# An encoder layer: order of expert loads, home of the one-hot tile, halves of a norm, place of the ranking, two slots, and steps of the attention list

## The chip, the cores and the metric

The kernel runs on one core of a Trainium2 chip. The metric is the device time of one execution in microseconds (us), as the median of three runs. Everything below speaks of the one core's engines: TensorE (PE; PEld is its loading of weights), VectorE (DVE), ScalarE (ACT), GpSimd (POOL), and SyncE (SP), on whose queue the loads of weights are issued.

## What is computed

One bidirectional encoder layer on 256 tokens of width 1024, in f32. From the reference, cut down:

```python
h = x @ w_in                                   # one projection, cut into six
qa, ka, va, qb, kb, vb = split(h)              # A: 8 heads on 2 kv heads; B: 4 differential heads
out_a = softmax(rope2d(rms(qa)) @ rope2d(rms(ka)).T / 8) @ va
p = softmax(rope(qb) @ rope(kb).T / 8)         # two maps per head
out_b = rms((p[:, :, 0] - lam * p[:, :, 1]) @ vb) * (1 - lambda_init)
x = LN(alpha * x + concat(out_a, out_b) @ w_mix_out)
x = LN(alpha * x + memory_cross_attention(x, mem, w_mem_q, w_mem_kv, w_mem_out))   # 4 heads, 256 memory tokens
logits = x @ w_router + b_router
top_v, top_i = top_k(logits, 4)                # 4 of 32 experts for each token
combine = one_hot(top_i) * softmax(top_v)
for e in range(32):
    g, u = x @ w_g[e] + b_g[e], x @ w_u[e] + b_u[e]        # 1024 x 1024 each
    g, u = min(g, 7), clip(u, -7, 7)
    y += combine[:, e] * ((g * sigmoid(1.702 * g) * (u + 1)) @ w_d[e] + b_d[e])
x = LN(alpha * x + y)
```

Each expert has three matrices of 4 MiB (gate, up, down), so the 32 experts are 384 MiB that must come from the chip's memory once.

## The kernel before

**Slots and pairs.** Weights stand in twenty places of 128 x 2048 f32 (1 MiB each), the slots; slots 2p and 2p + 1 together are pair p and can hold one load of 2 MiB. `free` (L117) lists the slots that are free, in the order in which they came free, at first 0 to 19. `take` (L132) takes the first of the list, `give` (L135) puts slots at its end, and `take_pair` (L141) takes the pair that has been complete for longest (`pairs`, L138). So the order of the list at the start, the order of the loads and the order in which tiles are used settle which load waits for which readers. Early work lies in slots too: the attention carves its tiles out of some, and other tiles come out of a slot named by hand. In the rows below, `sw` is a 1 MiB slot, `sp` a pair, `swh` and `srh` are half a slot with the projections' weights and their split parts.

**The loads.** There are two lists of loads in `queues` (L147 and on): the half loads of the projections, and the line of all other loads, which for the experts is put together at L336 to L340. For expert x it takes gate (`g_`), then the down matrix of the expert before (`d_`), then up (`u_`). `emit` (L207) gives a load its slot and issues it on SP, `pump` (L224) issues for as long as there is room. SP issues in order: a load whose slot is still being read holds all that stand behind it. The first two experts are fixed (NSTATIC = 2); their loads, and the gate and up of the third, are of 1 MiB, nearly all later ones of 2 MiB. Which experts come third and later is found at run time: they are ranked by the number of their tokens, and SP reads each rank's id with `values_load` (L332) before the first load of it. At the third expert (x == NSTATIC) the line before reads `*d_[:3], *g_, d_[3], *u_`: three down loads of expert 1, the four gate loads of the third, the fourth down load.

**The attention.** A planner is not used; the order of the attention's steps on TensorE, VectorE and ScalarE is written out by hand in `SEQ` (L49), one word for each step: `split` casts a weight tile and subtracts (on VectorE or, with G, on GpSimd), `proj,b..` is a projection, `rq` and `rB` are rotations of queries and keys, `rms` the reciprocal roots (L673), `qt` and `qB` and `kB` transpositions (L694), `S,c,h` scores and softmax exponentials (L700, L813), `N,c,h` the division of a block of scores by its sum (L705, L709), `T,c` the transposition of such a block with its copies (L712, L842 to L845), `V,c` the product with the values (L717, L722). Scores, transpositions and products share the four PSUM banks `ps` (L150), the projections four others (`pa`).

**The routing.** After the cross-attention, x2 (the tile `x_home`) is normed in two blocks of 128 tokens, `norm_part(c)` (L1063), one VectorE instruction each for all 1024 columns. `first_oh(c)` (L1087) makes the one-hot matrix that sorts a block's tokens to the first two experts; it is the tile `oh0` (L1085), half of a work tile `t`. `gather_part` (L1092) multiplies by it in two halves of 512 columns, each half into one bank, and `gather_out` (L1097) copies from the banks to `xgT`, the gathered tokens of the gate, in the place that the work tile `t` has. `rank_experts` (L1299) counts the tokens of each expert, six small matmuls on TensorE, and sorts; it is called once at L1321, ahead of the experts. `gate_part(0)` (L1462) is the first gate, 32 matmuls of L1285 in the order `FIRST`; `rank_ids` (L1334) behind it turns the ranks into ids, which SP waits for. Then the loop at L1464 goes through the experts: up, the next gate, down. `finish_routing` (L1166) makes the tables `posF` and `cmbF` for the later experts.

## Time and profile before

| what | value |
|---|---|
| three runs | 1138.49 to 1139.33 us, median 1138.79 us |
| profiled execution | 1140.94 us, with a span of 1139.2 us |
| TensorE busy | 1023.6 us, 90% of the span, 7603 matmuls |
| VectorE, ScalarE, GpSimd busy | 322.8, 231.9, 148.8 us |
| moved by DMA | 428.61 MB, mean 376 GB/s |
| expert loads of 2 MiB on SP | 57 down, 56 gate, 56 up |

The profile's busy times are averages over stages with different limits, so they are to be read by stage: the page has a row for the DMA engines in 40 slices of the span, and views of the trace give each engine's busy time for a window. A row of a timeline shows start, length, engine and line, the operation with output and input, the count, and in brackets how long the engine had been idle before it and what ended that. The profiled execution is one execution; its time stands beside the runs'.

### The profile page before, as it was taken

The numbers are of one execution on the slowest core, as the hardware profiler recorded it, in microseconds if no ns is written. First come the engines' busy times: TensorE is split into PE (matmuls) and PEld (weight loads), VectorE is DVE, ScalarE is ACT, GpSimd is POOL, SyncE is SP. The second block draws the span as 40 slices with busy tenths as digits, with TensorE's granted clock in tenths as the row PEclk, the third lists the DMA queues.
The fourth block names the chain that finished last, engine by engine and source line by source line (L and its number), as shares of the span: only waits on it lengthen the run. The fifth ranks groups of instructions, "written<-read, shape, count | busy, mean of one in ns | idle before, by whom it ended". The sixth has DMA issues, their size and how long they took to land. (4 is left out here: it accounts for less than half of the span.)

```text
span 1139.2 us, 18119 instructions
## 1 busy us (share of the span) xinstructions
PE 1023.6 (90%) x7603; PEld 537.5 (47%) x7603; DVE 322.8 (28%) x675; ACT 231.9 (20%) x472; POOL 148.8 (13%) x219
## 2 busy tenths in 40 slices
PE   9989999999986789899999899979898989889895
PEld 8768889863543334344444343424242323233232
DVE  6657794551210111121111112111111111102025
ACT  4846665420100101010111010101010101001020
POOL 6861030012110100020100000001010100000010
PEclk9989999999998999999999999999999999999977
DMA  8544558889999999999999999999999999999994
GB/s 265 201 135 165 164 192 323 344 334 405 379 426 426 427 425 429 426 427 426 427 426 426 427 425 429 427 428 426 428 428 427 428 426 429 427 427 427 428 426 186
DMA packets 50640, 428.61 MB, mean 376 GB/s; under 512 B 7063, under 2 KB 8376, under 8 KB 24700
## 3 DMA queue, kind: packets, MB, share of 16 engines
q1 hardware_dynamic: 50172, 426.11, 90.7%
q8 instruction: 61, 1.00, 0.4%
q0 software_dynamic: 384, 1.31, 0.3%
q14 instruction: 23, 0.19, 0.0%
HBM read 426.22 MB, written 1.18 MB: 375 GB/s over the span
## 5 line engine op out<-in xcount | busy, mean ns | idle before, releaser
L1285 PE MATMUL pa<-sp,xgT 128*32 128x256 f32 (+1 forms) x3264 | 391.1, 473 | 63.8 <-DMA sp<-in_w_e_up 32.7
L1285 PEld LDWEIGHTS pa<-sp,xgT 128*32 128x32 f32 (+1 forms) x3264 | 146.8, 121 | 279.4 <-issue 136.6
L1436 PE MATMUL pa<-sp,shared 128*32 128x256 f32 (+1 forms) x1696 | 191.8, 459 | 24.5 <-DMA sp<-in_w_e_down 16.5
L1436 PEld LDWEIGHTS pa<-sp,shared 128*32 128x32 f32 (+1 forms) x1696 | 72.9, 120 | 137.7 <-issue 81.1
L1402 POOL TENSOR_TENSOR shared<-shared,shared 128x512 f32<-128x512 f32 (+1 forms) x37 | 37.4, 1012 | 608.5 <-ACT shared L1399 608.5
L1428 ACT COPY shared<-pa 128x512 f32<-128x512 f32 (+1 forms) x37 | 17.8, 481 | 389.8 <-PE pa L1426 389.8
L1397 DVE TENSOR_SCALAR shared<-pa 128x512 f32<-128x512 f32 (+1 forms) x37 | 20.8, 562 | 200.9 <-PE pa L1285 200.9
L1416 DVE TENSOR_SCALAR shared<-pa 128x512 f32<-128x512 f32 (+1 forms) x37 | 20.8, 562 | 192.4 <-PE pa L1285 192.4
L248 DVE TENSOR_TENSOR srh<-swh,srh 128x1024 fp32r<-128x1024 f32 (+1 forms) x46 | 59.5, 1306 | 31.7 <-ACT srh L247 31.2
L247 ACT CAST srh<-swh 128x1024 fp32r<-128x1024 f32 (+1 forms) x59 | 60.1, 1037 | 22.6 <-PE pa L452 8.7
L1094 PEld LDWEIGHTS pa<-oh,x_home 128*128 128x128 f32 x416 | 47.4, 192 | 7.8 <-issue 7.8
L451 PE MATMUL pa<-srh,sr 128*128 128x512 f32 (+1 forms) x128 | 50.6, 398 | 0.0
L1094 PE MATMUL pa<-oh,x_home 128*128 128x128 f32 x416 | 49.9, 278 | 0.0
L452 PE MATMUL pa<-srh,sr 128*128 128x512 f32 (+1 forms) x128 | 49.4, 387 | 0.2 <-DVE sr L439 0.2
L453 PE MATMUL pa<-srh,sr 128*128 128x512 f32 (+1 forms) x128 | 49.1, 385 | 0.0
L1442 DVE COPY oa<-pa 32x256 f32<-32x256 f32 (+1 forms) x30 | 14.9, 496 | 112.6 <-ACT oa L1442 112.4
L1243 POOL TENSOR_SCALAR oh<-iota,pos 128x32 f32<-128x32 f32 (+1 forms) x70 | 26.6, 405 | 145.6 <-PE pa L1094 139.0
L1252 DVE TENSOR_SCALAR oc<-iota,pos,cmb 128x64 f32<-128x64 f32 (+1 forms) x74 | 19.0, 305 | 93.2 <-PE pa L1229 92.8
L1442 ACT COPY oa<-pa 32x256 f32<-32x256 f32 (+1 forms) x30 | 12.6, 420 | 133.0 <-PE pa L1436 128.5
L451 PE MATMUL pa<-sr,srh 128*128 128x256 f32 x128 | 37.6, 293 | 0.0
L453 PE MATMUL pa<-sr,srh 128*128 128x256 f32 x128 | 36.2, 283 | 0.0
L452 PE MATMUL pa<-sr,srh 128*128 128x256 f32 x128 | 36.2, 283 | 0.0
(368 smaller groups left out, 1064.9 us busy)
## 6 DMA issues: line engine op xcount, KB each, us to landing
sp<-in_w_e_down SPq DMA_DIRECT2D x57, 2048.0 KB
sp<-in_w_e_gate SPq DMA_DIRECT2D x56, 2048.0 KB
sp<-in_w_e_up SPq DMA_DIRECT2D x56, 2048.0 KB
sw<-in_w_e_up SPq DMA_DIRECT2D x12, 1024.0 KB
sw<-in_w_e_gate SPq DMA_DIRECT2D x10, 1024.0 KB
swh<-in_w_in SPq DMA_DIRECT2D x18, 512.0 KB
swh<-in_w_mem_kv SPq DMA_DIRECT2D x16, 512.0 KB
sw<-in_w_e_down SPq DMA_DIRECT2D x8, 1024.0 KB
```

The costliest lines, as they stand in the source:

```text
L247: S.copy(SRH[hi][h][:, m], SWH[raw][h][:, m])
L248: E.tensor_tensor(SRH[raw][h][:, m], SWH[raw][h][:, m], SRH[hi][h].bitcast(F32)[:, m], op=OP.subtract)
L451: T.matmul(ps, ah, bh, start=first, stop=False, skip_group_check=True)
L452: T.matmul(ps, al, bh, start=False, stop=False, skip_group_check=True)
L453: T.matmul(ps, ah, bl, start=False, stop=last, skip_group_check=True)
L1094: T.matmul(ps[h][:, 128 * k:128 * k + 128], x2[c][:, 512 * h + 128 * k:512 * h + 128 * k + 128], oh[:, c, :], start=(c == 0 and k == 0), s ...
L1243: G.tensor_scalar(oh[:, c, s0:s0 + m], iota[:, off:off + m], pos[:, c, col:col + 1], None, op0=OP.is_equal)
L1285: T.matmul(to(t), xgT[:, k, s0:s0 + n], cut(rows[k], t), start=False, stop=(k == order[-1]), skip_group_check=True)
L1397: V.tensor_scalar(gc, pv, LIMIT, None, op0=OP.min)
L1402: G.tensor_tensor(gc, gc, sg[:, 0:w], op=OP.mult)
L1436: T.matmul(p[n * t:n * t + n, 0:w], hT[:, 128 * j + n * b:128 * j + n * b + n], rows[kk][:, w * t:w * t + w], start=(kk == 0), stop=(kk == ...
L1442: eng(oa[s0:s0 + n, w * t:w * t + w], p[n * t:n * t + n, 0:w])
```

## The change

Six edits:

1. In `SEQ`, `N,2,1` and `N,2,0` stand ahead of `T,1` and the scores `S,3`, and `N,3,0` goes behind `qB,0`; `wr` goes behind the scores; and `rq,1` goes ahead of `rms`.
2. The entries 14 and 16 of `free` are exchanged at the start.
3. All four down loads of expert 1 stand ahead of the gate loads of the third expert.
4. The one-hot tile has a place of its own, `place0` of 128 x 256 f32, which `posF` and `cmbF` use later in place of two tiles.
5. The second block's norm is done in two halves of 512 columns, each just ahead of its half of the gather; the one-hot comes between.
6. `rank_experts` is called inside the first gate, behind the second of its eight rows of weights, in place of ahead of it.

```diff
@@ -49,10 +49,10 @@
 split,kv0,1,G split,bq0,0 split,bq0,1 proj,aq1,1 split,bq1,0 sqq,1 proj,kv0,0 rq,0 consts proj,kv0,1 sqk,1 sqk,0 split,bq1,1
-sqq,0 split,bk0,0,G proj,bq0,0 rk,1 va proj,bq0,1 rk,0 split,bk0,1,G rms rq,1 proj,bq1,0 proj,bq1,1 lam cols eq,0 kt
+sqq,0 split,bk0,0,G proj,bq0,0 rk,1 va proj,bq0,1 rk,0 split,bk0,1,G rq,1 rms proj,bq1,0 proj,bq1,1 lam cols eq,0 kt
 qt,0 split,bk1,0 qt,2 split,bk1,1,G split,bv0,0,G split,bv0,1,G proj,bk0,0 eq,1 S,0,0 S,0,1 S,1,0 rB,bq,1 S,1,1 N,0,0
 N,0,1 proj,bk0,1 T,0,V split,bv1,0,G S,2,0 N,1,1 S,2,1 N,1,0 split,bv1,1,G rB,bq,0 proj,bk1,0 split,k00,0 proj,bk1,1
-split,k00,1,G T,1 S,3,1 N,2,1 wr S,3,0 V,2 N,3,0 qB,0 N,2,0 split,k01,0 rB,bk,1 proj,bv0,0 proj,bv0,1 N,3,1 V,0 T,2
+split,k00,1,G N,2,1 N,2,0 T,1 S,3,1 S,3,0 wr V,2 qB,0 N,3,0 split,k01,0 rB,bk,1 proj,bv0,0 proj,bv0,1 N,3,1 V,0 T,2
 rB,bk,0 split,k01,1,G split,k10,0,G proj,bv1,0 qB,2 split,k10,1 proj,bv1,1 T,3 kB,0 vb mem V,3 M,4 M,2 V,1 M,0 M,6 ws
@@ -115,6 +115,7 @@
     free = list(range(SLOTS))
+    free[14], free[16] = 16, 14
@@ -336,7 +337,7 @@
         g_, d_, u_ = L_e[x][0], L_e[x - 1][2], L_e[x][1]
-        line += [*d_[:3], *g_, d_[3], *u_] if x == NSTATIC else [*g_, *d_, *u_]
+        line += [*d_, *g_, *u_] if x == NSTATIC else [*g_, *d_, *u_]
     queues[1][:] = line + L_e[-1][2]
@@ -1060,8 +1061,9 @@
-    def norm_part(c):
-        V.tensor_scalar(x2[c].rearrange("p (i e q) -> p i e q", i=2, e=KX), X1[c].rearrange("p (i q e) -> p i e q", i=2, e=KX),
+    def norm_part(c, i=slice(0, 2)):
+        V.tensor_scalar(x2[c].rearrange("p (i e q) -> p i e q", i=2, e=KX)[:, i],
+                        X1[c].rearrange("p (i q e) -> p i e q", i=2, e=KX)[:, i],
                         mv2[c][:, 0:1], sd2[c], op0=OP.subtract, op1=OP.mult)
@@ -1082,7 +1084,8 @@
-    oh0 = t512()[:, 0:256].rearrange("p (c s) -> p c s", c=2)
+    place0 = cst.tile([128, 256], F32)
+    oh0 = place0.rearrange("p (c s) -> p c s", c=2)
@@ -1135,12 +1138,14 @@
     route_part(1)
-    norm_part(1)
     route_count(1)
-    route_pos(1)
-    first_oh(1)
     for h in range(2):
-        gather_part(gps, 1, FIRST[4 * h] // 4, oh0)
+        i = FIRST[4 * h] // 4
+        norm_part(1, slice(i, i + 1))
+        if h == 0:
+            route_pos(1)
+            first_oh(1)
+        gather_part(gps, 1, i, oh0)
     give(s_x1)
@@ -1164,8 +1169,7 @@
     def finish_routing(keyc):
-        posF = cst.tile([128, 2, 2 * NE], F32)
-        cmbF = cst.tile([128, 2, 2 * NE], F32)
+        posF, cmbF = [place0[:, 128 * f:128 * f + 128].rearrange("p (c j) -> p c j", c=2) for f in range(2)]
         four = lambda t: t.rearrange("p c (j r) -> p c j r", j=2)
@@ -1264,7 +1268,7 @@
-    def gu(p, col, n, s0, xgT, b3_, rows, order=range(8)):
+    def gu(p, col, n, s0, xgT, b3_, rows, order=range(8), between=None):
         nb = 128 // n
@@ -1284,6 +1288,8 @@
                          start=False, stop=(k == order[-1]), skip_group_check=True)
+            if between and k == order[1]:
+                between()
         return p[:, 0:w]
@@ -1318,7 +1324,6 @@
-    keyc, posT = rank_experts()
     pinned.__exit__(None, None, None)
@@ -1384,14 +1389,14 @@
-    def gate_part(x):
+    def gate_part(x, between=None):
         col, jobs = seq[x]
         gather(x)
         rows = rows_in(L_e[x][0])
         for base, n in jobs:
             g, s0 = slot_of[x, base]
             p = pbank()
-            pv = gu(p, col, n, s0, xg[g], bg3, rows, FIRST if x == 0 else range(8))
+            pv = gu(p, col, n, s0, xg[g], bg3, rows, FIRST if x == 0 else range(8), between)
             w = pv.shape[1]
@@ -1459,7 +1464,9 @@
     ordered.__enter__()
-    gate_part(0)
+    ranks = []
+    gate_part(0, lambda: ranks.extend(rank_experts()))
+    keyc, posT = ranks
     rank_ids()
     for x in range(end):
         up_part(x)
```

TensorE's order in the attention, from T,1 (L842, transpositions of the block `shared_298`) to qB (L694, transpositions of `sw_67`), with the engines on which a row waits. Before:

```order
L842 MATMUL ps<-ident,shared_298 128x128 [waits DVE_49]
L842 MATMUL ps<-ident,shared_298 128x128 x3
...
L702 MATMUL ps<-kTA,sw_71 128x512 [waits Activation_49] x2
L722 MATMUL ps<-shared_297,vA 64x256 [waits DVE_49]
L722 MATMUL ps<-shared_297,vA 64x256 x3
L694 MATMUL ps<-ident,sw_67 128x128 [waits DVE_49,Pool_49]
L694 MATMUL ps<-ident,sw_67 128x128 x3
```

In the change:

```order
L843 MATMUL ps<-ident,shared_298 128x128 [waits DVE_49]
L843 MATMUL ps<-ident,shared_298 128x128 x3
...
L703 MATMUL ps<-kTA,sw_71 128x512 [waits DVE_49,PE_49]
L703 MATMUL ps<-kTA,sw_71 128x512 [waits DVE_49]
L723 MATMUL ps<-shared_297,vA 64x256 [waits Activation_49]
L723 MATMUL ps<-shared_297,vA 64x256 [waits DVE_49]
L723 MATMUL ps<-shared_297,vA 64x256
L723 MATMUL ps<-shared_297,vA 64x256 [waits Activation_49]
L695 MATMUL ps<-ident,sw_67 128x128 [waits PE_49,Pool_49]
L695 MATMUL ps<-ident,sw_67 128x128 x3
```

The matmuls stand in the same order; what they wait for differs. The scores waited for ScalarE and now wait for VectorE; qB waited for VectorE and GpSimd, and now for GpSimd and for a matmul of TensorE itself.

TensorE's order at the first gate, from the second block's gather (L1094, in the change L1097) over the ranking (L1302 to L1309, in the change L1308 to L1315) into the gate's rows of weights (`sw_77`, `sw_67`). Before:

```order
L1094 MATMUL pa<-t_2264,x_home 128x128 [waits DVE_49]
L1094 MATMUL pa<-t_2264,x_home 128x128 x7
...
L1302 MATMUL ps<-tri,maskb 32x256
...
L1307 MATMUL ps<-one_273,maskb 96x1
...
L1309 MATMUL ps<-maskb,one_273 96x32
...
L1285 MATMUL pa<-sw_77,xgT 64x512 [waits Activation_49]
...
L1285 MATMUL pa<-sw_67,xgT 64x512 [waits DMAHW0_49,Activation_49]
```

In the change:

```order
L1097 MATMUL pa<-place_2264,x_home 128x128 [waits DVE_49]
L1097 MATMUL pa<-place_2264,x_home 128x128 x3
L1097 MATMUL pa<-place_2264,x_home 128x128 [waits DVE_49]
L1097 MATMUL pa<-place_2264,x_home 128x128 x3
L1289 MATMUL pa<-sw_77,xgT 64x512 [waits Activation_49]
...
L1308 MATMUL ps<-tri,maskb 32x256
...
L1313 MATMUL ps<-one_273,maskb 96x1
...
L1315 MATMUL ps<-maskb,one_273 96x32
...
L1289 MATMUL pa<-sw_67,xgT 64x512 [waits DMAHW0_49,Activation_49]
```

The gather's second half has a wait of its own on VectorE, it reads the one-hot from `place`, and the ranking's matmuls stand between the gate's second row of weights, in `sw_77`, and its third, in `sw_67`.

SP's order at the expert ids (TENSOR_LOAD ids_i). `sw_58` to `sw_77` are slots 0 to 19, `sp_98` to `sp_107` pairs 0 to 9. Before:

```order
L219 DMA sw_77<-in_w_e_down 128x2048
L332 TENSOR_LOAD ids_i
...
L219 DMA sw_67<-in_w_e_gate 128x2048
...
L219 DMA sw_62<-in_w_e_gate 128x2048
L219 DMA sw_63<-in_w_e_down 128x2048
...
L219 DMA sp_98<-in_w_e_gate 128x4096
...
L219 DMA sp_99<-in_w_e_gate 128x4096
...
L219 DMA sp_101<-in_w_e_down 128x4096
```

In the change:

```order
L220 DMA sw_77<-in_w_e_down 128x2048
L220 DMA sw_67<-in_w_e_down 128x2048
L333 TENSOR_LOAD ids_i
...
L220 DMA sw_74<-in_w_e_gate 128x2048
...
L220 DMA sw_63<-in_w_e_gate 128x2048
...
L220 DMA sp_98<-in_w_e_gate 128x4096
...
L220 DMA sp_105<-in_w_e_gate 128x4096
...
L220 DMA sp_99<-in_w_e_down 128x4096
```

The fourth down load goes into slot 9 ahead of the read of the ids, the gate loads of the third expert go into slots 16, 8, 4 and 5, which held the first expert's up tiles, and the second 2 MiB gate load of the fourth expert goes into pair 7 (slots 14 and 15) in place of pair 1.

## Rows read from the trace of the kernel before

**Rows 1.** The profiled page: share of the DMA engines, 40 slices of 28.5 us

```profile
DMA  8544558889999999999999999999999999999994
```

**Rows 2.** Windows, 250 us to the stream's end: engines' busy, PEclk, DMA share, GB/s

```profile
250.00:260.00 10.00, 10.00 (x50) 3.21 (x48) 1.46 (x8) 0.76 (x2) 1.26 (x1) 1.00 0.63 223
...
280.00:290.00 10.00, 10.00 (x48) 4.13 (x45) 2.11 (x6) 0.00 (x0) 2.86 (x8) 0.83 0.71 263
...
290.00:1110.00 820.00, 729.69 (x5880) 314.49 (x5880) 129.93 (x289) 88.50 (x199) 63.07 (x109) 0.97 1.01 427
```

**Rows 3.** Timeline of SP's loads, 238 to 306 us: start, length, what, count

```profile
238.10 10.85 SPq L219 DMA_DIRECT2D sw<-in_w_e_down  x3
...
255.64 4.10 SPq L219 DMA_DIRECT2D sw<-in_w_e_gate  x4
...
261.12 0.34 SPq L219 DMA_DIRECT2D sw<-in_w_e_down  x1
...
263.06 5.48 SPq L219 DMA_DIRECT2D sw<-in_w_e_up  x4
...
273.21 13.67 SPq L219 DMA_DIRECT2D sp<-in_w_e_gate  x2
...
304.43 1.86 SPq L219 DMA_DIRECT2D sp<-in_w_e_gate  x2
```

**Rows 4.** Timeline of TensorE, Vector, Scalar, GpSimd, 58 to 85 us

```profile
58.15 1.44 DVE L248 TENSOR_TENSOR srh<-swh,srh 128x1024 fp32r<-128x1024 f32 x1 [2.71 <-ACT srh L247]
...
59.51 0.74 DVE L844 COPY shared<-ps 128x256 f32<-128x256 f32 x2
...
60.37 1.98 PE L702 MATMUL ps<-kTA,sw 128*128 128x512 f32 x4 [1.01 <-ACT shared L845]
...
62.34 0.88 DVE L709 TENSOR_SCALAR shared<-ps,rsm 128x256 f32<-128x256 f32 x2
...
63.27 1.08 PE L722 MATMUL ps<-shared,vA 128*64 128x256 f32 x8 [0.91 <-DVE shared L709]
...
65.48 0.36 ACT L438 CAST sr<-ps 128x256 fp32r<-128x256 f32 x1
...
66.45 1.09 PE L694 MATMUL ps<-ident,sw 128*128 128x128 f32 x4 [2.10 <-DVE rsm L831]
...
67.19 0.78 PE L451 MATMUL pa<-srh,sr 128*128 128x512 f32 x1
...
72.43 0.39 PE L451 MATMUL pa<-srh,sr 128*128 128x512 f32 x1
...
74.95 0.39 PE L453 MATMUL pa<-srh,sr 128*128 128x512 f32 x1
...
81.69 2.26 POOL L529 TENSOR_TENSOR t<-t,t 128x512 f32<-128x512 f32 x1
...
84.05 0.62 PE L694 MATMUL ps<-ident,t 128*128 128x128 f32 x4
```

**Rows 5.** The same window view, 65 to 75 us

```profile
65.00:75.00 10.00, 8.55 (x28) 6.94 (x28) 6.35 (x15) 1.79 (x4) 3.30 (x2) 0.66 0.10 31
```

**Rows 6.** Timeline of TensorE at 39 us

```profile
39.65 1.06 PE L694 MATMUL ps<-ident,t 128*128 128x128 f32 x8 [0.73 <-POOL t L527]
```

**Rows 7.** Timeline of the routing and the first gate, 243 to 254 us

```profile
243.99 2.05 PE L1094 MATMUL pa<-t,x_home 128*128 128x128 f32 x16 [1.00 <-DVE t L1088]
...
246.13 0.46 ACT L1104 ACTIVATE xgT<-pa,colsP 128x128 f32<-128x128 f32 x1 [2.10 <-PE pa L1094]
...
246.64 3.65 PE L1285 MATMUL pa<-sw,xgT 128*64 128x512 f32 x16
...
253.66 0.21 PE L1336 MATMUL pa<-perm,ecol 32*1 32x32 f32 x2
```

**Rows 8.** Timeline of TensorE behind the first down part

```profile
276.53 0.39 PE L1342 MATMUL pa<-ident,lgs 128*32 128x128 f32 x2
...
292.04 3.85 PE L1285 MATMUL pa<-sw,xgT 128*32 128x256 f32 x64
```

## The prediction

> **What bounds the kernel now.** I read the page first, then the kernel in stretches. The row of the DMA engines [rows 1] is ragged in its first nine slices and full from the tenth on, but for the last one: from 290 to 1110 us the share is 1.01 at 427 GB/s [rows 2]. In that stretch the expert weights set the time; TensorE is busy for 730 of its 820 us and follows them. So a microsecond that TensorE saves there is worth nothing, while a microsecond by which the stream gets to the same transfer earlier is worth one at the end. What can still be won lies ahead of 290 us, and there are two kinds of it.
>
> The first is holes in the stream after the experts began. From 250 to 260 us it moved 223 GB/s, from 280 to 290 us 263 GB/s [rows 2]; against 427 these are (1 - 223/427) x 10 = 4.8 and 3.8 us lost, 8.6 together: the most that filling them can bring. SP's loads say why [rows 3]. In the first hole the third down load of expert 1 ends its issue at 238.10 + 10.85 = 248.95, and nothing follows until 255.64, when SP has read the expert ids; the fourth down load, which needs no ids, stands behind four gate loads and goes at 261.12. In the second hole the second 2 MiB gate load of expert 3 is issued only at 273.21 + 13.67 = 286.88 at its end, since its pair holds two up tiles of expert 1.
>
> The second kind is TensorE's own delay before 250 us, where it is the engine that the loads wait for. Its waits there are few; the largest stand in one place of the attention and cost twice, since the granted clock falls behind them: 0.66 on the mean of 65 to 75 us [rows 5], so 2 x (1 - 0.66) x 10 = 6.8 us at 1.2 GHz.
>
> **The attention steps.** Before, TensorE ends T,1's transpositions at 60.37 - 1.01 = 59.4, the scores S,3 start at 60.37 after 1.01 us of waiting for Scalar's copy of T,1, V,2 at 63.27 after 0.91 us for N,2,1, and qB at 66.45 after 2.10 us [rows 4]. qB's bank is V,2's, which Vector frees behind Scalar's cast at 65.48, itself behind eight exponentials. In the change N,2,1 and N,2,0 free two banks ahead of S,3, and qB takes one that T,1 left: in the built order it waits for GpSimd and TensorE alone. Step by step: Vector's split ends at 58.15 + 1.44 = 59.6 [rows 4]; each N is 0.88 us [rows 4] and an estimated 0.2 for its reciprocal, so N,2,1 is done at 60.7 and N,2,0 at 61.75. S,3,1 runs from 60.7 to 61.7 and S,3,0 to 62.75 (1.98 us for two). T,1's copies come behind the Ns on Vector (0.74) and then on Scalar, done by about 62.9; V,2 (1.08) runs to 63.9, qB at the full clock 0.62 [rows 4], and the projection begins at 64.5 instead of 67.19: **2.7 us**.
>
> That projection is 24 matmuls. Before, it ran to 75.26, 8.1 us; behind 72.43 they start (74.95 - 72.43)/11 = 0.23 us apart [rows 4], so at the full clock it takes 5.5. TensorE's three waits between 59.4 and the projection, 1.01 + 0.91 + 2.10 = 4.0 us [rows 4], fall to an estimated 1.5, so I take the clock as kept: **2.6 us**. The bounds are 0 and 2.6. The Trainium skill, "TensorE: Matmul & The Clock Gate", section "A second HAM failure mode: psum-queue depth-cycling", says that short idles between groups that cycle through banks can be enough to make the clock swing between its two levels; by that the 2.6 us would be 0. The trace has one fall of the clock behind those three waits and can't tell their sum from their number, so it neither bears this out nor refutes it; as a rival it is (a).
>
> What is late next: Scalar's casts and Vector's copies come about 1 us later there, and kB's transpositions, which began at 84.05 directly behind GpSimd's addition (81.69 + 2.26 = 83.95) [rows 4], will meet it before it is done. With TensorE 5.3 us earlier and that addition some 4 to 5 us earlier I put the new wait between 0 and 1.2 us and take **0.7** off. Swapping rq,1 and rms takes away a wait of 0.73 us [rows 6], in which qt waited for rq,1's addition: GpSimd gets its operands before a split of its own instead of after; Scalar's chain lets most of it through, **0.6 us** (ends 0 and 0.73). wr moves on no engine. The part gives 2.7 + 2.6 - 0.7 + 0.6 = 5.2 us. From 75 to 245 us TensorE has hardly a wait, so I carry it to the end; the other end is a rival.
>
> **The routing.** Before, the second block's gather starts at 243.99 after 1.00 us of waiting and runs 2.05 us, to 246.04; Scalar's first copy of it has waited 2.10 us for all of it, though it needs only the first half, since it writes where the one-hot tile lay; the gate begins at 246.64 [rows 7]. With half of the norm now behind the one-hot, the gather can begin up to its wait of 1.00 us earlier; since the halves add an instruction and the first half still stands ahead, I take 0.3, so it runs 243.7 to 245.8; with its own home the first copies hide in its second half and the gate begins at 245.8. The six rank matmuls, in the gap of 0.6 us between 246.04 and 246.64, were covered; inside the gate they are not. So 0.8 us is gained and 0.65 given back: **0.15 us** (ends -0.6 and 0.8). The ids depend on the end of the gate, at 253.66 [rows 7], and move by the same 0.15. Vector has five microseconds for the ranks. posF and cmbF in the old one-hot tile cost nothing: its last reader, the first gather, is done before they are written.
>
> **The stream.** One load of 1 MiB takes 1.049/427 = 2.46 us, one of 2 MiB 4.91. From the 2.63 MB moved in 280 to 290 us, and nine loads of 1 MiB and one of 2 MiB ahead of the second hole [rows 3], both restarts come out 1.7 us behind their issue: 255.64 + 1.7 = 257.3; 257.3 + 9 x 2.46 + 4.91 = 284.4; the second at 288.2. In the change the fourth down load takes the slot whose gate tiles are read third and fourth; that is free at about 249.9 and the load fills 2.46 us of the first hole. The gate loads of expert 2 then follow the up tiles of expert 0 as they are read, from 255.5 on, always ahead of the stream. Eight loads remain: 257.2 + 8 x 2.46 + 4.91 = 281.8. The second gate half of expert 3 now goes to the pair of the third and fourth down tiles of expert 0, free when that down part ends, 276.5 [rows 8], so it runs 281.8 to 286.7. The next load needs the pair on which the gate half at 273.21 waited before, free about 286.5 [rows 3]: it starts at 288.1. There the stream is one 2 MiB transfer ahead: **4.9 us** (ends 0 and 8.6), and 1.4 us of hole are left. The next slots: gate 2 ends at 292.04 + 3.85 = 295.9 [rows 8], plus 1.7 is 297.6, the stream wants it at 288.1 + 2 x 4.91 = 297.9; the first gate half of expert 4 is free at 304.43 [rows 3], 306.1 with the 1.7, wanted at 307.7. Both hold, by 0.3 and 1.6 us.
>
> Sum: 5.2 + 0.15 + 4.9 = 10.25, say **10.3 us**. The profiled execution took 1140.94 us, with a span of 1139.2; it would take 1130.6. It lies 2.15 us above the median of the runs, 1138.79, so the median is forecast at **1128.5 us**.
>
> **Rivals.**
> (a) The clock still falls at 65 us: short idles remain in front of the projection, and one fall is on record there. For it: waits of 1.01 and 0.91 us came ahead of that fall, so the longest may not have been alone in it [rows 4]. Against it: TensorE's idle time there falls to less than half. Then 2.6 goes, and so does the wait of 0.7 at kB: gain 8.4, 1130.4 us.
> (b) The attention's gain is taken back before 245 us, by Vector or Scalar, whose work in 61 to 73 us does not get earlier. Gain 5.1, 1133.7 us.
> (c) The second hole stays: the exchange doesn't free a pair earlier, and then the first hole's 2.46 us is lost in the second, which grows. The built order speaks against it, the pair is another one. Gain 5.4, 1133.4 us.
> (d) Slower: with 5 us less of transfers waiting, the stream is 1.6 us from running dry at the gate of expert 4. If TensorE stays at 1.2 GHz from 280 to 304 us (it does so for 2 x 0.17 x 10 = 3.4 us of 280 to 290 now [rows 2]), it comes up to 20 us later, and the hole is 20 - 1.6 = 18: 1147 us. It decides from 12 us of lateness on, since 10.3 + 1.6 must be used up.
> (e) The change does less than it says: the one-hot's place still holds the copies, or SP is held by the fourth down load. The latter is free 4.6 us ahead of the ids. No change, 1138.8 us, if neither gain comes.
>
> **How the numbers follow.** Forecast 0.60, its own range 1126.5 to 1130; (a) 0.13; (b) 0.08; (c) 0.09; (d) 0.04; (e) 0.06. A measurement of this kernel can tell about 0.2%, 2.3 us, from no change: the first four are beyond it, so faster is 0.90, same 0.06, slower 0.04. The range runs from 1125.8, with the rest of the second hole (1.4), no wait at kB (0.7) and the routing's upper end (0.65 more), to 1133.7, which takes in (a), (b) and (c).
>
> **What would show it.** Right: qB starts about 2.6 us earlier against S,3 and the clock is 1.00 in 60 to 70 us; TensorE is at the first gather some 5 us earlier; the fourth down load's issue stands ahead of the ids; the DMA share dips only once, for 2 us, at the ids, and under 2 us at the up part of expert 1. Wrong: a clock of 0.5 in the values' projection, a new wait at kB over 1.2 us, a gate load of expert 3 issued 10 us behind the other, or a share under 1 behind 290 us.

## The result and the profile after

The changed kernel took 1131.76 us in the median of four runs (1128.90 to 1132.49), the kernel before 1139.06 (1138.49 to 1139.69, four runs as well): a ratio of 0.9929, 95% interval 0.9916 to 0.9941, so 7.3 us faster. The forecast was 1128.5 us and 10.3 us faster, with a range of 1125.8 to 1133.7. The direction holds, and the time lies in the range, though above the 1126.5 to 1130 that the prediction gave to its own forecast; the gain was overstated by 3 us. Beside the experiments below, on two different chips, the changed kernel took 1130.86 against 1141.26 (0.9916, 0.9903 to 0.9928) and 1131.23 against 1140.13 (0.9921, 0.9907 to 0.9934), which is 10.4 and 8.9 us faster.

The profiled execution of the change is the fastest of its four, 1128.90 us with a span of 1127.2, 12.0 less than the span shown of before. That is more than the medians give, and a good part of the study is about the difference. It is called the first profile of the change below.

The page's row of the DMA engines, and the window view with the columns of [rows 2]:

```profile
DMA  7545569899999999999999999999999999999994
```

```profile
65.00:75.00 10.00, 10.00 (x55) 7.79 (x54) 8.19 (x19) 5.21 (x10) 4.09 (x3) 1.00 0.62 190
240.00:255.00 15.00, 15.00 (x78) 4.92 (x76) 4.40 (x19) 2.37 (x3) 1.26 (x1) 1.00 0.90 324
250.00:260.00 10.00, 10.00 (x50) 3.35 (x48) 1.39 (x2) 0.00 (x0) 0.00 (x0) 1.00 0.95 358
280.00:290.00 10.00, 9.27 (x110) 6.17 (x110) 2.94 (x7) 2.62 (x6) 2.91 (x7) 1.00 1.01 428
```

The slices fill one slice earlier than in [rows 1]. In 250 to 260 us the stream moves 358 GB/s and in 280 to 290 us 428, where [rows 2] had 223 and 263. The clock of 65 to 75 us is 1.00 where [rows 5] had 0.66. The first hole ends 255.64 - 248.95 = 6.7 us earlier now, with the first gate load behind the ids ([rows 3], and the rows of SP below), and lies in 240 to 255 us, where 324 GB/s are (1 - 324/427) x 15 = 3.6 us lost. Before, it lay in 245 to 260 us and cost 5.6 us:

```profile
245.00:260.00 15.00, 15.00 (x80) 5.63 (x80) 4.71 (x20) 3.63 (x6) 1.26 (x1) 1.00 0.76 268
```

SP's loads in the timeline, as in [rows 3]:

```profile
231.51 12.13 SPq L220 DMA_DIRECT2D sw<-in_w_e_down  x4
248.95 5.48 SPq L220 DMA_DIRECT2D sw<-in_w_e_gate  x4
...
266.19 3.77 SPq L220 DMA_DIRECT2D sp<-in_w_e_gate  x2
277.82 2.05 SPq L220 DMA_DIRECT2D sp<-in_w_e_down  x2
```

All four down loads are one group now, issued by 231.51 + 12.13 = 243.64, ahead of the ids; the two 2 MiB gate loads of expert 3 (experts are counted from 0) end their issue at 269.96 and no longer at 286.88. The steps that the prediction named are all there.

TensorE in the attention, as in [rows 4], and qt, as in [rows 6]:

```profile
39.16 1.07 PE L695 MATMUL ps<-ident,t 128*128 128x128 f32 x8 [0.64 <-ACT sw L730]
...
60.00 2.02 PE L703 MATMUL ps<-kTA,sw 128*128 128x512 f32 x4 [1.16 <-DVE rsm L832]
61.95 1.08 PE L723 MATMUL ps<-shared,vA 128*64 128x256 f32 x8
...
63.38 0.48 PE L452 MATMUL pa<-srh,sr 128*128 128x512 f32 x1
...
69.04 1.08 PE L723 MATMUL ps<-shared,vA 128*64 128x256 f32 x8
...
78.23 0.66 PE L695 MATMUL ps<-ident,t 128*128 128x128 f32 x4 [0.25 <-POOL t L530]
```

Three waits became one of 1.16 us: V,2 and qB follow without any, the projection at 63.38 and not at 67.19, and it takes 69.04 - 63.38 = 5.66 us against 8.07. kB waits 0.25 us for GpSimd. qt waits 0.64 us against 0.73: what ends the wait is now a copy on ScalarE and no longer GpSimd's addition, and most of the wait has stayed.

The routing, as in [rows 7]:

```profile
233.60 2.03 PE L1097 MATMUL pa<-place,x_home 128*128 128x128 f32 x16
...
238.86 1.94 PE L1289 MATMUL pa<-sw,xgT 128*64 128x512 f32 x8
240.73 0.39 PE L1308 MATMUL ps<-tri,maskb 128*32 128x256 bf16 x2
...
246.63 0.21 PE L1341 MATMUL pa<-perm,ecol 32*1 32x32 f32 x2
```

The gate begins behind the gather without a gap and has the ranking in its middle. From the first block's gather to the gate's end it is 246.63 - 233.60 = 13.03 us, where before had 253.66 [rows 7] - 240.25 = 13.41, its first gather being

```profile
240.25 2.03 PE L1094 MATMUL pa<-t,x_home 128*128 128x128 f32 x16
```

### The profile page after: what moved, and what is told of

Same layout as the page of the kernel before. It is cut to its first block, busy times and chain, and to the rows that moved or that the text cites. A ratio compares the mean times of both kernels' runs of the same rounds, so it can differ in the third digit from the quotient of the medians.

```text
span 1127.2 us, 18118 instructions
## 1 busy us (share of the span) xinstructions
PE 1019.7 (90%) x7603; PEld 534.0 (47%) x7603; DVE 322.7 (29%) x676; ACT 232.0 (21%) x472; POOL 147.3 (13%) x219
## 4 chain that ended last, share of the span: by engine, by line
DMA 56%; PE 38%; DVE 2%; issue 1%; ACT 1%; POOL 1%; POOLq 0%; SPq 0%; ACTq 0%; DVEq 0%
DMA sp<-in_w_e_gate 24%; DMA sp<-in_w_e_down 18%; DMA sp<-in_w_e_up 14%; PE pa L1289 9%; PE pa L1441 7%; PE pa L453 4%; PE pa L452 4%; PE pa L454 4%; PE pa L1097 2%; PE ps L1268 2%; PE pa L1501 1%; PE ps L770 1%; ACT srh L248 1%; PE ps L964 1%; PE ps L983 1%
## 5 line engine op out<-in xcount | busy, mean ns | idle before, releaser
L1097 PEld LDWEIGHTS pa<-oh,x_home 128*128 128x128 f32 x416 | 47.4, 192 | 7.8 <-issue 7.8
L1097 PE MATMUL pa<-oh,x_home 128*128 128x128 f32 x416 | 49.9, 278 | 0.0
L452 PE MATMUL pa<-srh,sr 128*128 128x512 f32 (+1 forms) x128 | 49.6, 390 | 0.1
L453 PE MATMUL pa<-srh,sr 128*128 128x512 f32 (+1 forms) x128 | 48.4, 380 | 0.4 <-DVE sr L440 0.2
L454 PE MATMUL pa<-srh,sr 128*128 128x512 f32 (+1 forms) x128 | 48.2, 378 | 0.0
L452 PE MATMUL pa<-sr,srh 128*128 128x256 f32 x128 | 37.6, 294 | 0.0
L1404 ACT ACTIVATE shared<-shared 128x512 f32<-128x512 f32 (+1 forms) x37 | 19.6, 529 | 82.3 <-DVE shared L1402 82.3
L454 PE MATMUL pa<-sr,srh 128*128 128x256 f32 x128 | 36.2, 283 | 0.0
```

Of the source, the lines that this page charges most:

```text
L452: T.matmul(ps, ah, bh, start=first, stop=False, skip_group_check=True)
L453: T.matmul(ps, al, bh, start=False, stop=False, skip_group_check=True)
L454: T.matmul(ps, ah, bl, start=False, stop=last, skip_group_check=True)
L1097: T.matmul(ps[h][:, 128 * k:128 * k + 128], x2[c][:, 512 * h + 128 * k:512 * h + 128 * k + 128], oh[:, c, :], start=(c == 0 and k == 0), s ...
```

## The experiments

They ran in three groups (1 to 4, 5 to 8, 9 to 11) and a last run, each group on a chip of its own beside runs of before; the ratio to these is given, and its interval is some 1.5 us wide to either side. Differences in us are to the changed kernel of the first group, 1130.86; for runs 5 to 8 they go across two chips, so the difference of the two ratios, x 1140 us, is given too ("by the ratios").

**1. The changed kernel again** (no edit).

> The changed kernel unaltered. The two profiled executions lie 12.0 us apart in their spans (1139.2 and 1127.2), the medians of the runs only 7.3. Theory: what the change gains is the same in every execution but for the clock, and single executions of both kernels differ by a clock fall of 2 to 3 us in one place; then a second profiled execution near 1131 to 1132 us shows the same start of the gate (238.9) and the same loads, and differs from the first in one stretch where the granted clock is 0.5, or in a hole of the stream. Rival: the first profiled execution was fast in the stream itself (a higher GB/s from 290 us on); then the second has the same clock and the difference grows evenly behind 290 us.

Measured: 1130.86 us (1130.53 to 1132.68). The first theory holds, but for the gate, which started 0.6 us later (239.47 against 238.86); 0.4 of that stood already at 39 us (qt at 39.58 against 39.16). Here the granted clock fell behind the start of expert 1's up part, which takes 8.73 us for 32 matmuls, as in the profile of before; in the first profile of the change it took 7.03. TensorE's timelines:

```profile
279.49 8.73 PE L1285 MATMUL pa<-sw,xgT 128*64 128x512 f32 x32
```

```profile
272.46 7.03 PE L1289 MATMUL pa<-sw,xgT 128*64 128x512 f32 x32
```

```profile
273.07 8.73 PE L1289 MATMUL pa<-sw,xgT 128*64 128x512 f32 x32
```

```profile
274.00:276.00 2.00, 2.00 (x6) 0.47 (x4) 0.37 (x3) 0.00 (x0) 2.00 (x6) 0.50 1.04 442
280.00:295.00 15.00, 14.27 (x134) 7.92 (x132) 3.39 (x7) 2.63 (x6) 2.90 (x7) 1.00 0.99 394
```

The first row is of the profile of before, the second of the change's first profile, the rest are the timeline and windows of this run's profile: the clock is 0.50 at 274 to 276 us, and 280 to 295 us then move 394 GB/s, where the first profile had 428 in 280 to 290. That is (1 - 394/427) x 15 = 1.2 us of stream lost, and most of the 1.9 us between the two spans.

**2. Without the attention's steps.** `SEQ` as before, the rest of the change kept.

> The changed kernel with the old list of the attention's steps, all else of the change kept. Theory: the attention's gain is carried one for one to the end, so this is 5.2 us (as forecast) to 6.6 us (as the start of the first gather moved between the two traces) slower than the changed kernel, about 1137.5 us, and the clock falls at 65 us as before. Rival (b): it is taken back before 245 us; then it is under 1.5 us slower.

Measured: 1135.38 us (1134.86 to 1137.69), 0.9958 (0.9945 to 0.9971): 4.5 us slower (4.8 by the ratios). Rival (b) is out; the gain is carried to the end (the first gather starts 238.73 - 234.21 = 4.5 us later than in run 1's profile, and the span is 4.5 us longer), but it is 4.5 and not 5.2 to 6.6. TensorE's timeline and the windows:

```profile
39.57 1.07 PE L695 MATMUL ps<-ident,t 128*128 128x128 f32 x8 [0.80 <-POOL t L528]
...
66.35 0.63 PE L695 MATMUL ps<-ident,sw 128*128 128x128 f32 x4 [2.11 <-DVE rsm L832]
...
74.03 1.08 PE L723 MATMUL ps<-shared,vA 128*64 128x256 f32 x8
```

```profile
65.00:70.00 5.00, 3.65 (x14) 2.96 (x15) 4.15 (x10) 1.69 (x4) 1.89 (x1) 0.77 0.00 0
70.00:75.00 5.00, 5.00 (x24) 3.48 (x22) 2.11 (x6) 0.00 (x0) 1.30 (x1) 0.89 0.35 105
```

qB's wait is that of before, and the clock falls again, but for a shorter time (0.77 and 0.89; before had 0.66 over the ten us): the projection runs from 66.73 to 74.03, 7.3 us and not 8.07. How long the fall lasts differs from execution to execution: the seventh run's profile, with the same order of the divisions, has 74.53 - 66.47 = 8.06 us again.

**3. Without the stream's steps.**

```diff
-    free[14], free[16] = 16, 14
-        line += [*d_, *g_, *u_] if x == NSTATIC else [*g_, *d_, *u_]
+        line += [*d_[:3], *g_, d_[3], *u_] if x == NSTATIC else [*g_, *d_, *u_]
```

> The changed kernel with the old order of the fourth down load and the two slots not exchanged. Theory: both holes come back and cost 4.9 us, so about 1136.7 us, with the down load behind the ids and the second gate half of the fourth expert some 10 us behind the first. Rival (c): the second hole is not tied to the exchange and only the first returns: 2.5 us at most, about 1134 us.

Measured: 1135.79 us (1133.90 to 1135.84), 0.9950 (0.9937 to 0.9963): 4.9 us slower (3.9 by the ratios), as the theory has it. SP's gate loads of expert 3, the second of which ends its issue only at 280.20, and the stream in the first hole:

```profile
266.56 13.64 SPq L219 DMA_DIRECT2D sp<-in_w_e_gate  x2
```

```profile
240.00:255.00 15.00, 15.00 (x78) 4.98 (x76) 4.52 (x19) 2.63 (x4) 1.26 (x1) 1.00 0.79 285
```

**4. Without the routing's steps**: ranking ahead of the gate, one-hot in the work tile, norm in one piece.

> The changed kernel with the ranking ahead of the gate, the one-hot tile in the work tile and the norm of the second block in one piece. Theory: 0.15 us (forecast) to 0.4 us (the gate's end moved by 7.03, the first gather's start by 6.65) slower, not to be told from no change. Rival: the three steps are worth the whole 1.13 us by which the gate's start moved beyond the first gather's, since the ranking hides behind other waits.

Measured: 1130.75 us (1129.16 to 1132.93), 0.9910 (0.9895 to 0.9924): no difference.

```profile
234.39 2.03 PE L1096 MATMUL pa<-t,x_home 128*128 128x128 f32 x16
...
240.28 3.65 PE L1287 MATMUL pa<-sw,xgT 128*64 128x512 f32 x16
...
247.30 0.21 PE L1340 MATMUL pa<-perm,ecol 32*1 32x32 f32 x2
```

From the first gather to the gate's end it is 12.91 us, against 13.03 with the steps. With them the gate starts 238.86 - 233.60 = 5.26 us behind the first gather and not 240.28 - 234.39 = 5.89, and it takes 7.77 us and not 7.02, since the ranking is inside it: 0.63 us are gained and 0.75 given back.

**5 and 6. The two steps of the stream apart.** The fifth run has the order of the change without the line `free[14], free[16] = 16, 14`; the sixth has the exchange with the old order `*d_[:3], *g_, d_[3], *u_`.

> The changed kernel without the exchange of slots 14 and 16; the four down loads still stand ahead of the ids. Theory, as in the prediction's rival (c): what the first hole gives is lost again in the second, which waits for TensorE's up part of expert 1 whatever lies ahead of it, so this is as slow as the changed kernel without both steps: 4.5 to 5 us slower than the changed kernel. Rival: the two steps add up; then only the second hole is back, about 2.5 to 3 us slower.

> The changed kernel with the old order of the fourth down load, the exchange kept. Theory: only the first hole is back. It lost 5.6 us by GB/s in the 15 us from 245 us before and 3.6 us in the change (240 to 255 us), so 2.0 to 2.5 us slower than the changed kernel. Rival: behind the exchange the stream is bound by the pair that the next down load needs (the up tiles of expert 1), so that an earlier stream only waits there: under 0.7 us slower.

Measured: without the exchange 1134.88 us (1132.28 to 1136.43), 0.9946 (0.9932 to 0.9960), 4.0 us slower (3.4 by the ratios); with the old order of the down load 1130.85 us (1130.43 to 1132.88), 0.9922 (0.9909 to 0.9935), no difference by the medians and 0.0006 x 1140 = 0.7 us by the ratios. So in the times the exchange is worth nearly the whole, and the first hole next to nothing. It is not that the hole wasn't there, in the windows of the sixth:

```profile
240.00:255.00 15.00, 15.00 (x78) 5.00 (x76) 4.52 (x19) 2.47 (x4) 1.26 (x1) 1.00 0.77 281
280.00:295.00 15.00, 14.27 (x134) 7.96 (x134) 3.15 (x7) 2.63 (x6) 2.91 (x7) 1.00 1.01 430
```

240 to 255 us move 281 GB/s against 324 with the step, which is (324 - 281)/427 x 15 = 1.5 us, but the span is 1129.1 us, that of run 1's profile of the full change. In this execution the up part of expert 1 took 7.03 us and the stream went through 280 to 295 us at 430 GB/s; in run 1's profile, 1.5 us further on, it waited there and lost 1.2. Against the first profile of the change, whose up part took 7.03 us too, the sixth run does stay behind: the second half of its last down part but one starts at 1095.13 us, there at 1093.75 (the row stands with the tail below), 1.4 us earlier.

```profile
1095.13 1.93 PE L1441 MATMUL pa<-sp,shared 128*32 128x256 f32 x32 [0.32 <-DMA sp<-in_w_e_down]
```

As far as these three profiles show, the slots that the up part frees set a bound of their own: what is won ahead of it is kept where TensorE's clock holds there and mostly lost where it falls. The fifth run shows the bound without slack:

```profile
266.16 13.67 SPq L219 DMA_DIRECT2D sp<-in_w_e_gate  x2
```

```profile
272.44 8.73 PE L1288 MATMUL pa<-sw,xgT 128*64 128x512 f32 x32
```

```profile
275.00:280.00 5.00, 5.00 (x24) 1.59 (x22) 0.00 (x0) 0.00 (x0) 0.73 (x3) 0.90 0.18 75
```

The second gate load waits until 279.83 and 275 to 280 us move 75 GB/s. Here a slower up part goes straight into the hole, and the six runs spread over 4 us. All three profiles without the exchange (before, runs 3 and 5) have the fall of the clock in that up part, of the eight others that have the exchange and not the eighth run's step only two do. Whether the exchange also makes the fall rarer is not shown; if it does, a part of its 3.4 to 4.0 us is the clock's.

**7. Without the divisions' new places.** `rq,1 rms` kept, the rest of `SEQ` as before.

> The changed kernel with the old places of the divisions N,2 and N,3 and of wr; rq,1 still ahead of rms. Theory after the second experiment: the wait of qt is 0.64 to 0.74 us in the change against 0.73 before, so the exchange of rq,1 and rms gives nothing and the divisions give all of the attention's gain: 4.5 us slower than the changed kernel, as without all of the attention's steps. Rival (the prediction's term): 0.6 us of the 4.5 belong to rq,1 and this is 3.9 us slower; qt's wait would then tell, since the times can't.

Measured: 1135.53 us (1132.79 to 1136.37), 0.9952 (0.9939 to 0.9966): 4.7 us slower than the change (4.1 by the ratios), and within 0.2 of the second run, which has the old `rms rq,1` as well.

```profile
39.16 1.07 PE L695 MATMUL ps<-ident,t 128*128 128x128 f32 x8 [0.55 <-ACT sw L730]
```

qt waits 0.55 us with rq,1 first, and 0.55 to 0.86 in the eleven other profiles that have it so (the median of the twelve is 0.57); without it 0.73 in the profile of before and 0.80 in the second run's. So some 0.2 us of the wait went with it, and the times can't tell even that: against the second run this one is 0.15 us slower by the medians and 0.7 faster by the ratios. Which of qt's operands is last has changed, and hardly when it is there.

**8. The tables inside the up part of expert 1.**

```diff
-        if x == 0:
-            combT = rank_finish(posT)
+        if x == 1:
+            steps = rank_finish(posT)
+            up_part(1, lambda k: parts.append(next(steps)))
```

> The changed kernel with the work behind the first down part (ten small matmuls that turn ranks into tables, 2.7 us of TensorE with waits of 0.15 and 0.51) moved into the up part of expert 1, behind its first, second and fourth rows of weights; nothing is left out. Theory: executions differ by whether the granted clock falls at that up part (it fell in the profiled executions of before, of the changed kernel's second look and of the one without the stream's steps, each time behind these waits, and costs 1.7 us there). Without the waits it doesn't fall, the up tiles come free 2 to 4 us earlier, and the kernel's executions lie closer together and near the fastest: 1129 to 1130 us. Rival: the spread comes from elsewhere (start, stream); then the median is that of the changed kernel, 1130.9, and the spread stays at 2 us. A third way: the gather behind the up part now waits for GpSimd's one-hot tiles, 1 to 2 us, and nothing is won.

Measured: 1130.08 us (1129.47 to 1131.30), 0.9908 (0.9893 to 0.9922): the lowest median, but 0.8 us below the change (0.9 by the ratios) is less than these runs can tell. In the timeline the work stands between the rows of weights, without a wait, and the window of these 10 us has the full clock:

```profile
271.07 0.39 PE L1347 MATMUL pa<-ident,lgs 128*32 128x128 f32 x2
...
272.40 0.63 PE L1355 MATMUL pa<-perm,posT 32*128 32x32 f32 x4
...
275.27 0.60 PE L1364 MATMUL pa<-one_col,inside 128*128 128x1 f32 x4
```

```profile
270.00:280.00 10.00, 10.00 (x55) 4.13 (x52) 3.37 (x15) 1.15 (x3) 4.95 (x14) 1.00 1.03 437
```

The clock held in this and in two later profiles with the step, and fell in five of the eleven without it (before among them). That fits the theory; three profiles don't prove it. And the profiled execution, with as full a stream as the fastest one of the change, took 1131.30 us: it lost its time at the other place, in the tail (35.5 us from the second half of the last down part but one to the end, where the first profile of the change has 1127.2 - 1093.75 = 33.45).

**9 to 12. The tail.** The ninth run is the change once more; the tenth adds extra matmuls where TensorE waits near the end, the eleventh the eighth run's step too.

```diff
+    def idle(p, m):
+        for i in range(m):
+            T.matmul(p, ident, gb3[:, 0, 0:512], start=True, stop=True)
...
+    idle(pbank(), 7)
     pump()
```

> The changed kernel once more, as the partner of the next two on the same chip. Theory: its executions lie between 1128.9 and 1132.7 us as they did before, and what sets an execution apart is the clock of two places, the up part of expert 1 (7.0 or 8.7 us) and the tail behind the last down load (33.4 us from that load's second half to the end in the fastest, up to 35.7 in others). Rival: the profiled execution shows both at their short values and is still above 1130.

> The changed kernel with twelve extra matmuls of 128x512 whose results nobody reads, where TensorE waits near the end: three between the halves of the last down part but one, seven ahead of the loop that follows the experts, two ahead of the small matmul behind it. Theory: in the changed kernel's profile the granted clock is 0.5 to 0.65 from 1104 to 1112 us, and the last up part takes 5.18 us (5.05 to 6.25 in the other profiles) where 64 such matmuls take 3.83 at the full clock. If the extra matmuls keep the clock, 1.3 to 2.4 us go: 1128.5 to 1129.5 us against 1130.9. Rival: they delay the loop's barrier or the small matmul by as much as they bring, or the clock falls all the same; then no change or 1 us slower.

> Both: the tables inside the up part of expert 1 and the extra matmuls near the end. Theory: the two places of the clock that set executions apart are both taken care of, so this is the fastest, 1127.5 to 1128.5 us, with the smallest spread (under 1 us). Rival: as the changed kernel, 1130.9.

Measured: 1131.23 (1130.07 to 1132.35), 1133.29 (1131.71 to 1134.35; 0.9943, 0.9930 to 0.9957) and 1134.21 us (1132.72 to 1134.64; 0.9943, 0.9930 to 0.9957). The ninth, profiled at 1132.20 us, needed 8.27 us for the up part of expert 1 and 1130.4 - 1096.49 = 33.9 in the tail, 1.24 and 0.5 more than the first profile. These are 1.7 of the 3.2 us between the two spans, so its theory, by which the two places set an execution apart, is borne out for half of the difference; the other half was not traced. The extra matmuls made the kernel slower, by 2.1 us for the tenth run against the ninth. TensorE in the tail, of the change and of the tenth run:

```profile
1093.75 1.93 PE L1441 MATMUL pa<-sp,shared 128*32 128x256 f32 x32 [1.52 <-DMA sp<-in_w_e_down]
...
1096.70 3.67 PE L1524 MATMUL ps<-oa,sc 96*128 96x512 f32 x8 [0.65 <-DVE oa L1447]
1104.57 1.08 PE L1630 MATMUL pa<-sw,oh 128*32 128x256 f32 x8 [4.19 <-PEq L1544]
...
1108.53 5.18 PE L1289 MATMUL pa<-sp,xgT 128*32 128x256 f32 x64
...
1115.83 3.66 PE L1441 MATMUL pa<-sp,shared 128*32 128x256 f32 x64 [0.46 <-ACT shared L1433]
```

```profile
1096.86 3.67 PE L1530 MATMUL ps<-oa,sc 96*128 96x512 f32 x8 [0.66 <-DVE oa L1453]
1100.37 6.17 PE L1438 MATMUL pa<-sw,ident 128*128 128x512 f32 x14
1106.84 0.64 PE L1637 MATMUL pa<-sw,oh 128*32 128x256 f32 x8 [0.30 <-PEq L1551]
...
1110.10 3.85 PE L1289 MATMUL pa<-sp,xgT 128*32 128x256 f32 x64
...
1116.93 5.35 PE L1445 MATMUL pa<-sp,shared 128*32 128x256 f32 x64 [0.46 <-ACT shared L1433]
```

The clock did hold, and the last up part took 3.85 us where it had 5.18. But the seven matmuls (two passes each, 14 in the row) ran 6.17 us, 0.88 each, in a gap of 4.19; the work behind the loop began 9.98 us after the start of the sums (the row of L1530, in the change L1524) and not 7.87; and the last down part then ran 5.35 us, against 3.66 in the change, so the clock was lost there instead. The eleventh run's profile has the same 9.98 and 5.35. The twelfth run mends the size, has Vector take the up part first, and keeps the eighth's step:

> The changed kernel with the tables inside the up part of expert 1 (as in the eighth run), shorter extra matmuls of 128x256 (0.44 us each, half of the 0.88 that those of 128x512 took, which held the loop's barrier up by 2.2 us): eight ahead of the loop in a gap of 4.1 us, two ahead of the small matmul behind it (gap 1.18), two behind the last up part; and VectorE clamps the last up part's result before it does the statistics and the centring of the second 128 rows (2.7 us) and not behind them. Theory: the last up part takes 3.85 us as in the tenth run, and what follows no longer waits for VectorE's 2.7 us; the tail behind the last down load but one, 33.4 to 35.7 us in the profiles, comes to 31.5 to 32.5, and the kernel to 1127.5 to 1129 us. Rival: the barrier or the last down part's clock takes it back, and it is within 0.7 us of the eighth run's 1130.1.

Measured: 1132.19 us (1129.78 to 1136.57), 0.9923 (0.9909 to 0.9936). In its profiled execution, the slowest of the seven:

```profile
1099.41 3.67 PE L1533 MATMUL ps<-oa,sc 96*128 96x512 f32 x8 [0.61 <-DVE oa L1453]
1102.92 3.62 PE L1440 MATMUL pa<-sw,ident 128*128 128x256 f32 x16
1109.43 1.08 PE L1640 MATMUL pa<-sw,oh 128*32 128x256 f32 x8 [2.89 <-PEq L1554]
```

Here the extra matmuls ended 1106.54 - 1099.41 = 7.1 us behind the start of the sums, early enough for the 7.87 of the change, and still the work behind the loop began 10.0 us after it. Why stays open. Its theory failed: the last up part took 4.58 us and not 3.85, and the tail 1134.8 - 1094.86 = 39.9 us, where 31.5 to 32.5 were expected. No version here beats the change beyond doubt; the eighth is the only candidate.

## Why the prediction was right in direction and 3 us too high

**The attention, forecast 5.2.** Worth 4.5 us by run 2 and 4.7 by run 7 (4.8 and 4.1 by the ratios). From the end of T,1's transpositions to the projection it was 67.19 - 59.36 = 7.83 us [rows 4] and is 63.38 - (60.00 - 1.16) = 4.54, 3.3 gained where I had 2.7; run 1's profile has 4.56. The scores started 1.16 us behind the transpositions, where I had put 60.7 - 59.36 = 1.34, and from their start to the projection it was 63.38 - 60.00 = 3.38 us, where I had 64.5 - 60.7 = 3.8. The projection gave 2.4 against the forecast 2.6 in the shown pair of profiles, and against the seventh run's, but only 7.3 - 5.66 = 1.6 against the second's: a fall of the clock is not a fixed price. The clock stayed at 1.00 there in all eleven profiles that have the new places, behind one wait of 1.14 to 1.19 us, and fell in all three with the old ones, behind three waits; rival (a) is out. By the rule from the Trainium skill's "TensorE: Matmul & The Clock Gate", section "A second HAM failure mode: psum-queue depth-cycling", the 2.6 would have been 0; the groups cycle through the same banks as before, so that alone did not bring the clock down here. The short idles that the section names with it are mostly gone in the change, so the rule is not refuted. Whether the sum of the waits, their number or the longest of them counts, these runs don't tell. The wait at kB was 0.24 to 0.29 us and not 0.7. Between the profiles of run 2 and run 1, taken on one chip, the three parts are (66.73 - 59.25) - 4.56 = 2.9, 1.6 and -0.3 us, 4.2 together, of the 4.5 by which the first gather moved; so of the 5.2 it is the price of the clock that was put too high, by 1.0. **The term for rq,1 failed**: 0.6 us forecast, some 0.2 us of the wait gone and nothing that the times can tell. I had read the wait's releaser [rows 6] as its only cause; with it out of the way a copy on Scalar ends the wait at nearly the same time. The 0.5 us by which qt starts earlier in the first profile of the change come for the most part from the start of the kernel: the first 32 transpositions took 6.61 us before, 5.65 in that profile and 6.49 in run 1's, where qt starts within 0.1 us of before.

**The routing, forecast 0.15.** Nothing, as the fourth run shows; the working had the right parts, 0.8 gained and 0.65 given back, and they measured 0.63 and 0.75.

**The stream, forecast 4.9.** Worth 4.9 by the third run (3.9 by the ratios), but **the step that splits it failed**. I had counted a filled first hole at 2.46 us by itself and let the second follow. Runs 5 and 6 have 3.4 to 4.0 for the exchange and 0 to 0.7 for the down load. The bound I had named with 1.4 us of hole left, the pair that the up tiles of expert 1 hold, takes back an earlier stream when that up part is slow. This is rival (d) in small: TensorE at 1.2 GHz for some 3.4 us and not 24, and a cost of 1.2 us in the hole and not 18. Rival (c) is out: the second hole did go. One reading in the working is off as well: the restart at 288.2 lies 288.2 - 286.88 = 1.3 us behind its issue and not 1.7; with 1.7 at both restarts the term would have been some 5.3, further from what was measured.

**The sum and its base.** 4.5 + 0 + 4.9 = 9.4 us from the single steps (4.8 + 0 + 3.9 = 8.7 by the ratios), against 10.3; the three comparisons gave 7.3, 10.4 and 8.9 (8.1, 9.6 and 9.0 by the ratios). So the 3 us are not firm themselves: the forecast gain was too high by nothing to 3 us. What separates the comparisons, and the 12.0 of the two profiles, is in good part the clock in two places that differ from execution to execution: the up part of expert 1 (7.03 to 8.73 us) and the tail (33.2 to 35.7 without extra matmuls). The profile of before has the fall at the first place, ahead of a hole that waits for just that up part, so up to 8.73 - 7.03 = 1.7 us of the 3.8 that I read from 280 to 290 us can belong to the execution. **The base is the step that I take to have failed: I put the 2.15 us between that execution and the median outside the sum, and most of them seem to have lain in the hole that I was filling**: an execution of before without the fall would have some 1.7 us less to win there. The four runs of before in the first comparison (1138.5 to 1139.7) are at the low end of the eleven beside the first experiments (1139.0 to 1142.1), where the change won the 10.4. With the 1.7 and the 0.75 for rq,1 and the routing taken off, 10.3 comes to 7.9, and 7.3 was measured. This is argued and not shown: no profile of a run of before at the low end was taken, and all three profiles without the exchange have the fall.

**The range.** 1131.76 us lies above the 1126.5 to 1130 of the forecast itself, and so do 1130.86 and 1131.23. The stated range went up to 1133.7 to take in rivals (a), (b) and (c), and none of the three came: that the time lies in it is owed to its width, and in that part it is luck.

## What to carry to other kernels

Before a hole in a stream is priced, find whether the slot behind it is late by the transfers or by the engine that reads it: here a gap that was filled ahead of a bound set by the reader was worth 0 to 0.7 us of a possible 2.5, and sending one load to another slot 3.4 to 4.0. A wait's releaser is the last of several operands; ask when the one before it was there. And look at two or three executions before taking a single one's clock as a property of the kernel: 1.7 us here came and went with it.

## What the runs showed that I had not expected

The same program loses TensorE's clock in some executions and keeps it in others, at the same place: 7.03 and 8.73 us for the same 32 matmuls in two profiles of the change. Extra matmuls ahead of the closing loop, 3.62 or 6.17 us in all, moved what follows it by about the same: it began 9.98 to 10.02 us behind the start of the sums in the three profiles that have them, and 7.65 to 8.24 in the eleven that don't.
